# The memory's values first, the residual and the memory's parts kept in DRAM, and the first output units by heads

## The chip, the cores and the metric

The kernel runs on one core of a Trainium2 chip. The metric is the device time of one execution, in microseconds. Engines are named as the profile names them: PE (TensorE matmuls), PEld (its weight loads), DVE (VectorE), ACT (ScalarE), POOL (GpSimd), SP (SyncE, which issues the DMAs here). Each engine works through its own instructions in program order and waits on semaphores for the others.

## The reference

One layer over 256 tokens of width 1024: a mixer of four branches, a cross-attention into 256 memory tokens, and a mixture of 32 experts, each followed by a layer norm of alpha times the residual plus the branch.

```python
h = layer_norm(x, ln0)                       # "LN0"
z = h @ w_in + b_in                          # 36 column blocks of 256
h = layer_norm(alpha*h + mixer(z) @ w_out + b_out)
q = h @ ca_wq;  k = mem @ ca_wk;  v = mem @ ca_wv
o = softmax(q k^T / sqrt(256)) v             # 4 heads of 256
h = layer_norm(alpha*h + o @ ca_wo)
h = layer_norm(alpha*h + moe(h))             # top 4 of 32 experts
```

The values v depend only on the memory and on ca_wv, on nothing that the layer computes before.

## The kernel before

**Units.** All dense products before the experts are a queue of units (class `Unit`, L142). A unit is one weight block of 1024 x 256: `load` (L147) issues its 1 MiB on SP into one of three raw buffers; `split` (L153) makes the high part by an ACT cast (L162) and the low part as raw minus high, the first 640 columns of 2048 on POOL (L164) and the other 1408 on DVE (L166), into one of three ring slots W0 to W2. The run is 48 matmuls in two halves: high by high (L135), high by low (L137), low by high (L139), each over 8 k-blocks.

**Order.** `step` (L197) drives the queue: before unit i it issues the load of unit i+4 and the split of unit i+3 at the latest, and between the halves `advance` lets every chain (a generator with the elementwise work of a branch) go one yield further. What stands in an engine's row is fixed when the program is built; a load on SP that waits for its buffer holds all DMAs behind it.

**Stages.** The front: x is loaded, LN0 runs on DVE and ACT, 16 transposes (L235) bring it to columns, parts hT_hi and hT_lo are made, and the first in-unit starts. The mixer: 36 in-units and 8 branch units beside the chains of the branches. The middle: `chain_mem` (L851) loads memT, x again and three broadcast rows (ln0_g, ln0_b, b_out), splits memT into memT_hl (slot X), and rebuilds the residual h: subtract and scale on DVE (L861), times ln0_g (L862) and plus ln0_b (L864) on POOL, times alpha plus b_out on DVE (L868). Then the units k0, out0 to out3, k1 to k3, q0 to q3, v0 to v3 (L902), o0 to o3 (L922). `chain_att` (L1186) does one head: scores (L1192), max (L1195), exponentials (L1197), normalization (L1199), then, once that head's values are there, the transposes of the probabilities (L1206) and the product with the values vm (L1214), whose parts go to oT_hl (slot A).

**Experts.** Their weights, 128 tiles of 2 MiB (L1051) and 128 of 1 MiB (L1060), come over the same SP queue into rings of big slots (E, X, W1, W2, W0, A) and small slots (f, k, m, raw0, raw1, v, n, b), each as soon as its slot is free. `load_experts(2)` after the first attention steps issues one big tile into E and one small one into f; `load_experts(3)` four steps later goes on with X.

```python
    step(4)
    load_experts(2)
    step(4)
    load_experts(3)
```

Of the kernel before, what the change touches and what calls it, by code (L numbers as in the profile page):

```python
# [7 lines left out]
F32 = mybir.dt.float32  # L8
F32R = mybir.dt.float32r
# [11 lines left out]
NT = 2  # L21
# [30 lines left out]
def hybrid_layer_kernel(ctx: ExitStack, tc: tile.TileContext, t, dbg=None):  # L52
# [19 lines left out]
    def slot(where, shape, name, dt=F32):  # L72
        return slots[where].tile(shape, dt, tag=where, name=name)
# [6 lines left out]
    def by_k(pair):  # L80
        return tuple(a.rearrange("p (k t) -> p k t", k=KD) for a in pair)
# [9 lines left out]
    xs = ctx.enter_context(ExitStack())  # L91
    xp = xs.enter_context(tc.tile_pool(name="xp", bufs=1, side="right"))

    xt = [xp.tile([P, D], F32, tag="xt", bufs=2, name=f"xt{i}") for i in range(NT)]
    for i in range(NT):
        S.dma_start(xt[i], xrow[:, i, :])
    cols = cp.tile([P, NCOL], F32, name="cols")
# [44 lines left out]
    class Unit:  # L142
# [151 lines left out]
    prime(1, 0)  # L294
    S.dma_start(cols, t["cols"])
    prime(2, 0)
# [9 lines left out]
    norm(xt[1], *mr0[1])  # L306
    prime(2, 1)
    to_cm(xt[0], 0, hTf, "ln0g", "ln0b")
    to_cm(xt[1], 1, hTf, "ln0g", "ln0b", lambda: pz.tile([P, 4, P], F32, tag="z", name="ps_tr"))
# [5 lines left out]
    A.activation(warm, eps, AF.Sigmoid)  # L315
    xs.close()
# [485 lines left out]

    NMIX = len(queue)

    def until(n):
        step(n - st_["done"])
# [4 lines left out]
    chains.append(chain_b0())  # L811
    until(4)
    pms[:] = [(pmm, "mm")]
    conv[0] = chain_conv()
    chains.append(conv[0])
    until(7)
    chains.append(chain_c())
    until(16)
    chains.append(chain_d())
    until(18)  # L820
    sil_ready.append(1)
    merged = slot("m", [P, KD, T], "merged")
    until(20)
    xc_.close()
# [16 lines left out]
    def bcast(name):  # L841
        o = p3.tile([P, D], F32, tag="bcast", name="bc_" + name, bufs=4)
        S.dma_start(o, t[name].rearrange("(o d) -> o d", o=1).to_broadcast([P, D]))
        return o

    mf = slot("f", [P, KD, T], "memT_f")
    mx = mTh, mTl = by_k(hi_lo("X", "memT_hl"))
    h = slot("h", [P, NT, D], "h")
    st1 = [p3.tile([P, 4, 6], F32, tag="st", bufs=4, name=f"st1{n}") for n in range(NT)]

    def chain_mem():  # L851
        S.dma_start(mf, t["memT"])
        S.dma_start(h, xrow)
        g0, b0, bo = bcast("ln0_g"), bcast("ln0_b"), bcast("b_out")
        for q in range(4):
            yield
            yield
            sl = slice(2 * q, 2 * q + 2)
            split(mf[:, sl, :], mTh[:, sl, :], mTl[:, sl, :])
            if q < 2:  # L860
                V.tensor_scalar(h[:, q, :], h[:, q, :], *mr0[q], ALU.subtract, ALU.mult)  # L861
                G.tensor_tensor(h[:, q, :], h[:, q, :], g0, ALU.mult)  # L862
            else:
                G.tensor_tensor(h[:, q - 2, :], h[:, q - 2, :], b0, ALU.add)  # L864
        yield
        for n in range(NT):
            yield
            V.scalar_tensor_tensor(h[:, n, :], h[:, n, :], ALPHA, bo, ALU.mult, ALU.add)  # L868

# [31 lines left out]

    def unit_v(q):  # L902
        def run(w):
            ps = psum()
            tm(ps, 0, w, mx, KD)
            yield
            tm(ps, 1, w, mx, KD)
            V.tensor_copy(vm[:, :, q * 256:(q + 1) * 256], ps)
            v_done.append(q)
        queue.append(Unit(t["ca_wv"][q], KD, 256, run))  # L910

    def half(ps, n, w, ks, first, last):
# [9 lines left out]
    def unit_o(q):  # L922
        def run(w):
            ps = [psum()[:, 0, :] for _ in range(NT)]
            if q == 0:

                half(ps[0], 0, w, range(6), True, False)
                yield
                half(ps[1], 1, w, range(6), True, False)
                for n in range(NT):  # L930
                    half(ps[n], n, w, range(6, 8), False, True)
                    eva_o(q, n, ps[n])
            elif q == 1:
                for n in range(NT):
                    half(ps[n], n, w, range(8), True, True)
                    eva_o(q, n, ps[n])
                    if n == 0:
                        yield
            elif q == 2:
# [242 lines left out]
    qT = slot("m", [P, KD, T], "qT")  # L1182
    v_done = []
    oT = []

    def chain_att(hd):  # L1186
# [12 lines left out]
        V.tensor_tensor(pr, pr, sm[:, :, None].to_broadcast([P, NT, T]), ALU.mult)  # L1199
        while hd not in v_done:  # L1200
            yield
        pt = p3.tile([P, 2, T], F32, tag="pt", name="pt", bufs=2)
# [14 lines left out]

    step(4)
    load_experts(2)
# [543 lines left out]
```

## Time and profile before

| | |
|---|---|
| median of 3 runs | 1427.59 us (1427.23 to 1428.79) |
| profiled execution | 1427.23 us, of which the span of the trace 1425.5 us |
| PE busy | 1263.8 us (89%) |
| DVE, ACT, POOL busy | 531.7, 314.2, 232.7 us |
| mean DMA rate over the span | 338 GB/s, 482.04 MB in all |
| first in-unit's first matmul | 14.02 us |
| attention's V units | 419.69 to 450.60 us |
| first expert tile into a unit's ring slot (W1) issued | 466.90 us |

The span is cut into stages by what they wait for: up to about 465 us PE is nearly always busy and DMA is not, from there to the end DMA is full and PE is not. Groups of rows below are cited by number; a "window" is a stretch of the span with each engine's busy time in it, PEclk is the granted TensorE clock (1.00 is 2.4 GHz, 0.50 is 1.2 GHz).

### The profile page before, as it was taken

Reading aid. Unit: us, or ns where it says so; the run is one execution under the profiler, and the core shown is the slowest. Engines: PE = TensorE matmul, PEld = TensorE weight load, DVE = VectorE, ACT = ScalarE, POOL = GpSimd, SP = SyncE. Lnnn points to the kernel's source line nnn. Section 1 sums busy time; section 2 is a strip of 40 time slices with the busy share of each in tenths; the row PEclk is TensorE's granted clock in tenths of the full one; section 3 lists DMA queues with packets and bytes.
Section 4 is the critical chain, followed back from the end, with each engine's and each line's share of the span. In section 5 each row is a group of like instructions: output and inputs, shape, how many; then the busy total and the mean of one; then the engine's idle time right before and its main releaser. Section 6 shows DMA issues by size and latency. Waiting matters only on the chain. (4 is left out here: it accounts for less than half of the span.)

```text
span 1425.5 us, 18505 instructions
## 1 busy us (share of the span) xinstructions
PE 1263.8 (89%) x7677; PEld 739.9 (52%) x7677; DVE 531.7 (37%) x830; ACT 314.2 (22%) x433; POOL 232.7 (16%) x143
## 2 busy tenths in 40 slices
PE   6999999989999999877999799799899978976764
PEld 6989898978999743311443343344244322322111
DVE  5587779978944522111031121121113111211113
ACT  4475574453643300000000000000000000000001
POOL 6233144559653200000000000000000000000000
PEclk9999999998999999988999999999899998999987
DMA  6353334556575999999999999999999999999994
GB/s 235 119 178 119 119 119 163 187 227 203 182 271 211 385 429 405 424 423 425 427 425 425 424 423 427 425 426 424 425 427 425 425 424 425 426 425 426 424 420 204
DMA packets 51979, 482.04 MB, mean 338 GB/s; under 512 B 7840, under 2 KB 8240, under 8 KB 10704
## 3 DMA queue, kind: packets, MB, share of 16 engines
q1 hardware_dynamic: 51888, 480.79, 82.6%
q8 instruction: 62, 1.02, 0.3%
q14 instruction: 29, 0.24, 0.0%
HBM read 479.72 MB, written 1.05 MB: 337 GB/s over the span
## 5 line engine op out<-in xcount | busy, mean ns | idle before, releaser
L1471 PE MATMUL ps_h<-w,xg 128*32 128x512 f32 (+2 forms) x2048 | 418.3, 638 | 64.2 <-DMA w<-in_moe_w 59.5
L1471 PEld LDWEIGHTS ps_h<-w,xg 128*32 128x32 f32 (+2 forms) x2048 | 133.6, 134 | 325.0 <-issue 219.0
L1534 PE MATMUL ps_y<-w,at 128*32 128x512 f32 (+2 forms) x1024 | 214.2, 631 | 38.0 <-DMA w<-in_moe_w 37.4
L1480 DVE TENSOR_SCALAR act<-ps_h 128x512 f32<-128x512 f32 (+1 forms) x36 | 24.7, 687 | 497.9 <-PE ps_h L1471 497.8
L164 POOL TENSOR_TENSOR w_hl<-w_f,w_hl 128x640 fp32r<-128x640 f32 (+1 forms) x64 | 162.3, 2540 | 226.0 <-ACT w_hl L162 213.1
L1676 POOL TENSOR_TENSOR r<-r,gb 128x512 f32<-128x512 f32 x2 | 3.0, 1492 | 926.5 <-ACT r L1675 926.5
L1534 PEld LDWEIGHTS ps_y<-w,at 128*32 128x32 f32 (+2 forms) x1024 | 62.8, 133 | 166.9 <-issue 83.7
L166 DVE TENSOR_TENSOR w_hl<-w_f,w_hl 128x1408 fp32r<-128x1408 f32 x63 | 117.4, 1866 | 69.1 <-ACT w_hl L162 66.1
L162 ACT CAST w_hl<-w_f 128x2048 fp32r<-128x2048 f32 x63 | 120.0, 1906 | 103.9 <-DMA w_f<-in_w_in 36.0
L1518 ACT COPY ta<-ps_sc 128x256 f32<-128x256 f32 (+1 forms) x32 | 11.8, 369 | 472.8 <-PE ps_sc L1516 472.8
L379 DVE SCALAR_TENSOR_TENSOR convacc<-u,cols,convacc 128x256 f32<-128x256 f32 x120 | 90.2, 752 | 2.5
L135 PE MATMUL ps_mm<-hT_hi,w_hl 128*128 128x256 f32 x512 | 74.7, 289 | 5.5 <-ACT hT_hi L311 2.3
L1555 PE MATMUL acc<-y,ta 32*128 32x512 f32 (+2 forms) x256 | 73.6, 641 | 5.0 <-DVE y L1544 4.0
L139 PE MATMUL ps_mm<-hT_hi,w_hl 128*128 128x256 f32 x512 | 73.7, 287 | 2.5 <-POOL w_hl L164 1.8
L137 PE MATMUL ps_mm<-hT_lo,w_hl 128*128 128x256 f32 x512 | 74.0, 288 | 0.0
L135 PEld LDWEIGHTS ps_mm<-hT_hi,w_hl 128*128 128x128 f32 x512 | 66.9, 193 | 8.5 <-issue 3.1
L139 PEld LDWEIGHTS ps_mm<-hT_hi,w_hl 128*128 128x128 f32 x512 | 67.6, 196 | 3.2 <-POOL w_hl L164 2.2
L137 PEld LDWEIGHTS ps_mm<-hT_lo,w_hl 128*128 128x128 f32 x512 | 67.6, 196 | 0.6 <-DVE hT_lo L314 0.6
L1342 PEld LDWEIGHTS ps_g<-sg,h 128*128 128x128 f32 x416 | 50.5, 198 | 12.2 <-issue 8.3
L1342 PE MATMUL ps_g<-sg,h 128*128 128x128 f32 x416 | 53.0, 286 | 0.3
L1481 ACT ACTIVATE sg<-act 128x512 f32<-128x512 f32 (+1 forms) x36 | 22.7, 631 | 135.3 <-DVE act L1480 134.1
L1555 PEld LDWEIGHTS acc<-y,ta 32*128 32x128 f32 (+2 forms) x256 | 26.0, 194 | 30.8 <-issue 19.1
(397 smaller groups left out, 1242.8 us busy)
## 6 DMA issues: line engine op xcount, KB each, us to landing
w<-in_moe_w SPq DMA_DIRECT2D x128, 2048.0 KB, 29.4
w<-in_moe_w SPq DMA_DIRECT2D x128, 1024.0 KB, 29.5
w_f<-in_w_in SPq DMA_DIRECT2D x36, 1024.0 KB, 4.9
w_f<-in_w_branch SPq DMA_DIRECT2D x8, 1024.0 KB, 4.9
w_f<-in_ca_wk SPq DMA_DIRECT2D x4, 1024.0 KB, 4.9
w_f<-in_w_out SPq DMA_DIRECT2D x4, 1024.0 KB, 5.0
w_f<-in_ca_wq SPq DMA_DIRECT2D x4, 1024.0 KB, 5.0
w_f<-in_ca_wv SPq DMA_DIRECT2D x4, 1024.0 KB, 4.9
```

Source lines behind the costliest of these rows:

```text
L135: PE.matmul(out, wh(i), xh(i), start=first and i == ks[0], stop=False)
L137: PE.matmul(out, wh(i), xl(i), start=False, stop=False)
L139: PE.matmul(out, wl(i), xh(i), start=False, stop=last and i == ks[-1])
L162: A.copy(hi, self.raw)
L164: G.tensor_tensor(lo[:, :n], self.raw[:, :n], hi.bitcast(F32)[:, :n], ALU.subtract)
L166: V.tensor_tensor(lo[:, n:], self.raw[:, n:], hi.bitcast(F32)[:, n:], ALU.subtract)
L379: V.scalar_tensor_tensor(ca[:, c, :], u[:, c, j:j + T], col("caw", 4 * j + c), ca[:, c, :], ALU.mult, ALU.add)
L1342: PE.matmul(pss[k // 4][:, k % 4 * w:(k % 4 + 1) * w], h[:, n, feature_tile(0, k)], sg[:, n, :w], start=n == 0 and k % 4 == 0, stop=n == N ...
L1471: PE.matmul(up_out(cap, hp_, m, i), x[:, k, :], w[:, c:c + 512], start=False, stop=k == KD - 1, skip_group_check=True)
L1480: V.tensor_scalar(g, hg, LIMIT, None, ALU.min)
L1534: PE.matmul(o, at[:, k, :], w[:, q * 512:(q + 1) * 512], start=k < (2 if cap == 32 else 1), stop=k >= KD - (2 if cap == 32 else 1), skip_g ...
L1555: PE.matmul(acc[n][q], a, b, start=False, stop=last, skip_group_check=True)
```

## The change

Line numbers of the new kernel are given as L.. "after". The memory's transpose is loaded first of all, in two halves, then wv0, x, the column constants, wv1, wv2, the three broadcast rows; memT is split at once, its parts are stored to DRAM (s_mem, 2 MiB, L329 after). The queue begins with the four V units; they run as steps 1 to 4 between the parts of LN0: V0, V1, the transposes, V2, V3, then in0. Each V unit's result is copied by ACT and stored to s_v (L305 after). The residual is finished here (POOL times ln0_g L344, plus ln0_b L352; DVE L353) and stored to s_h (L354 after). `chain_mem` is gone; the middle loads h, memT_hl and, later, vm from DRAM (4 MiB where it was 3.5 MiB). The attention has no V units between q3 and o0. The big ring begins X, A, W1, W2, W0, E, and oT_hl lies in E; `load_experts(2)` stands four steps earlier. Unit o0 does o0 and o1 together, by heads: k-blocks 0 to 3, then 4 and 5, then 6 and 7 of both.

```diff
+    s_mem = dp.tile([P, 2, KD * T], F32, name="s_mem")
+    s_v = dp.tile([P, NT, D], F32, name="s_v")
+    s_h = dp.tile([P, NT, D], F32, name="s_h")
+    mf = xp.tile([P, KD, T], F32, name="memT_f")
+    for i in range(2):
+        S.dma_start(mf[:, 4 * i:4 * i + 4, :], t["memT"][:, 4 * i:4 * i + 4, :])
...
+    def unit_v(q):
+        def run(w):
+            ps = psum()
+            tm(ps, 0, w, mx, KD)
+            yield
+            tm(ps, 1, w, mx, KD)
+            vs = xp.tile([P, 2, T], F32, tag="vs", name="vs", bufs=2)
+            A.copy(vs, ps)
+            S.dma_start(s_v[:, :, q * 256:(q + 1) * 256], vs)
+        queue.append(Unit(t["ca_wv"][q], KD, 256, run))
...
+    for q in range(4):
+        unit_v(q)
     for q in range(2):
         unit_in(q, eva_v(q))
...
+    for q in range(4):
+        sl = slice(2 * q, 2 * q + 2)
+        split(mf[:, sl, :], mTh[:, sl, :], mTl[:, sl, :])
+    prime(3, 1)
+    S.dma_start(s_mem, mhl.bitcast(F32))
+    step(1)
...
+    step(1)
     to_cm(xt[0], 0, hTf, "ln0g", "ln0b")
...
+    for n in range(NT):
+        G.tensor_tensor(xt[n], xt[n], row0[0], ALU.mult)
+    step(1)
...
+    for n in range(NT):
+        G.tensor_tensor(xt[n], xt[n], row0[1], ALU.add)
+        V.scalar_tensor_tensor(xt[n], xt[n], ALPHA, row0[2], ALU.mult, ALU.add)
+        S.dma_start(s_h[:, n, :], xt[n])
+    step(1)
...
+    S.dma_start(h, s_h)
+    S.dma_start(mhl.bitcast(F32), s_mem)
...
-    def chain_mem():
...
+    S.dma_start(vm, s_v)
...
-    big = ["E", "X", "W1", "W2", "W0", "A"]
+    big = ["X", "A", "W1", "W2", "W0", "E"]
...
-        while hd not in v_done:
-            yield
+        yield
...
+                part(range(4), parts[:1])
                 yield
...
+                part(range(4), parts[1:])
+                advance()
+                part(range(4, 6), parts[:2])
+                advance()
+                part(range(4, 6), parts[2:])
+                part(range(6, 8), parts)
...
-    step(4)
     load_experts(2)
     step(4)
     load_experts(3)
```

Three places show how this orders the instructions. First SP at the start of the program, before, down to the first small constants (wlr):

```order
L96 DMA xt_78<-in_x 128x1024
L96 DMA xt_79<-in_x 128x1024
L151 DMA w_f<-in_w_in 128x2048
L295 DMA cols<-in_cols 128x292
L151 DMA w_f<-in_w_in 128x2048 x3
L351 DMA wlr<-in_w_lr 128x128
```

And SP of the changed kernel, from the store of the memory's parts on (memT, x, the columns, wv0 to wv2 and the rows stand ahead of it):

```order
L329 DMA s_mem<-memT_hl 128x4096
L157 DMA w_f<-in_ca_wv 128x2048
L305 DMA s_v<-vs 256x1x256
L157 DMA w_f<-in_w_in 128x2048
L305 DMA s_v<-vs 256x1x256
L157 DMA w_f<-in_w_in 128x2048
L305 DMA s_v<-vs 256x1x256
L354 DMA s_h<-xt_86 128x1024
L354 DMA s_h<-xt_87 128x1024
L157 DMA w_f<-in_w_in 128x2048
L305 DMA s_v<-vs 256x1x256
L157 DMA w_f<-in_w_in 128x2048
```

The load of the third in-unit's weights (the third `in_w_in`) now stands behind both stores of the residual. Second, POOL at the start, before: one split, then the constants.

```order
L164 TENSOR_TENSOR w_hl<-w_f,w_hl 128x2048
L321 MEMSET ones 128x128
L323 MEMSET nones 128x128
L325 AFFINE_SELECT ntri<-nones 128x128
L328 CAST identb<-ident 128x128
```

And POOL of the changed kernel at the same place:

```order
L169 TENSOR_TENSOR w_hl<-w_f,w_hl 128x640 x4
L344 TENSOR_TENSOR xt_86<-xt_86,bc_ln_g 128x1024
L344 TENSOR_TENSOR xt_87<-xt_87,bc_ln_g 128x1024
L169 TENSOR_TENSOR w_hl<-w_f,w_hl 128x640
L352 TENSOR_TENSOR xt_86<-xt_86,bc_ln_b 128x1024
L352 TENSOR_TENSOR xt_87<-xt_87,bc_ln_b 128x1024
L169 TENSOR_TENSOR w_hl<-w_f,w_hl 128x640
L361 MEMSET ones 128x128
```

The four V units' splits and the residual's four operations stand ahead of the constants, between them the splits of in0 and in1. Third, SP in the attention, before:

```order
L151 DMA w_f<-in_ca_wq 128x2048 x4
L151 DMA w_f<-in_ca_wv 128x2048 x3
L1051 DMA w_4277<-in_moe_w 128x4096
L1060 DMA w_4279<-in_moe_w 128x2048
L151 DMA w_f<-in_ca_wv 128x2048
L151 DMA w_f<-in_ca_wo 128x2048 x3
L1051 DMA w_4561<-in_moe_w 128x4096
L151 DMA w_f<-in_ca_wo 128x2048
```

And in the changed kernel:

```order
L157 DMA w_f<-in_ca_wq 128x2048 x3
L1068 DMA w_4257<-in_moe_w 128x4096
L1077 DMA w_4259<-in_moe_w 128x2048
L157 DMA w_f<-in_ca_wq 128x2048
L157 DMA w_f<-in_ca_wo 128x2048 x3
L1068 DMA w_4553<-in_moe_w 128x4096
L157 DMA w_f<-in_ca_wo 128x2048
```

The first two expert tiles (3 MiB) stood ahead of the last V unit's weights; now they stand ahead of the last q unit's.

## Rows read from the trace of the kernel before

**Rows 1.** Busy time by window: `us, PE (x) PEld DVE ACT POOL, PEclk, DMA share, GB/s`
```profile
445.00:450.00 5.00, 5.00 (x38) 4.79 (x37) 2.26 (x2) 0.59 (x1) 2.97 (x1) 1.00 0.01 3
...
600.00:1400.00 800.00, 692.26 (x3446) 261.07 (x3446) 136.47 (x269) 50.70 (x95) 0.00 (x0) 0.95 1.01 425
```

**Rows 2.** Timeline of SP's issues, attention: start, us, engine, line, op, tile, [idle <-releaser]
```profile
392.70 3.24 SPq L151 DMA_DIRECT2D w_f<-in_ca_wq  x2
...
451.23 0.37 SPq L151 DMA_DIRECT2D w_f<-in_ca_wo  x1
...
466.90 0.43 SPq L1051 DMA_DIRECT2D w<-in_moe_w  x1
```

**Rows 3.** Timeline of the first 30 us, columns as in rows 2
```profile
8.35 3.33 PE L235 MATMUL ps_tr<-ident,xt 128*128 128x128 f32 x16 [8.35 <-DVE l0rs L124]
...
9.04 1.04 ACT L158 CAST w_hl<-w_f 128x1024 fp32r<-128x1024 f32 x1 [1.38 <-DMA w_f<-in_w_in]
...
14.02 0.74 PE L135 MATMUL ps_mm<-hT_hi,w_hl 128*128 128x256 f32 x4 [2.35 <-ACT hT_hi L311]
...
14.63 0.20 POOL L321 MEMSET ones<- 128x128 f32 x1
...
15.58 1.22 PE L135 MATMUL ps_mm<-hT_hi,w_hl 128*128 128x256 f32 x4 [0.82 <-DVE hT_hi L311]
...
22.71 3.11 POOL L164 TENSOR_TENSOR w_hl<-w_f,w_hl 128x640 fp32r<-128x640 f32 x2
...
23.95 1.12 PE L135 MATMUL ps_mm<-hT_hi,w_hl 128*128 128x256 f32 x8
```

**Rows 4.** A window in the first unit, columns as in rows 1
```profile
18.00:19.00 1.00, 1.00 (x5) 0.97 (x5) 1.00 (x1) 1.00 (x1) 1.00 (x2) 0.50 0.93 374
```

**Rows 5.** The four V units' matmuls in their window, columns as in rows 1
```profile
419.69:450.60 30.91, 24.83 (x192) 23.42 (x192) 0.00 (x0) 0.00 (x0) 1.00 0.51 197
```

**Rows 6.** Timeline, POOL's part of a split, without DVE beside it and with
```profile
37.70 1.57 POOL L164 TENSOR_TENSOR w_hl<-w_f,w_hl 128x640 fp32r<-128x640 f32 x1 [1.87 <-ACT w_hl L162]
...
306.70 2.99 POOL L164 TENSOR_TENSOR w_hl<-w_f,w_hl 128x640 fp32r<-128x640 f32 x1 [2.18 <-ACT w_hl L162]
```

**Rows 7.** Operations on tile h, middle stage: duration ns min/median/max, starts
```profile
L862 POOL TENSOR_TENSOR h<-h,bc_ln_g x2: 2403/3042/3680, 302.1 to 314.6; 128x1024 f32<-128x1024 f32 x2
...
L864 POOL TENSOR_TENSOR h<-h,bc_ln_b x2: 2814/2834/2853, 320.7 to 326.4; 128x1024 f32<-128x1024 f32 x2
```

**Rows 8.** PE's waits, 300 to 345: waited for, us in total, times, longest
```profile
PE ps_mm L135 <- ACT merged_hl L128: 2.8, 2, 1.6
...
PE ps_mm L137 <- DVE yl L129: 2.7, 1, 2.7
```

**Rows 9.** Windows of the middle stage, columns as in rows 1
```profile
320.00:324.00 4.00, 3.81 (x19) 3.52 (x18) 4.00 (x2) 0.00 (x0) 4.00 (x3) 0.50 0.52 168
...
344.00:348.00 4.00, 4.00 (x20) 4.00 (x20) 2.18 (x3) 1.86 (x2) 3.71 (x13) 0.50 0.98 258
```

**Rows 10.** Timeline of the attention, ACT, DVE, POOL and PE, columns as in rows 2
```profile
397.57 1.90 ACT L162 CAST w_hl<-w_f 128x2048 fp32r<-128x2048 f32 x1 [6.68 <-DMA w_f<-in_ca_wq]
...
400.61 1.90 ACT L162 CAST w_hl<-w_f 128x2048 fp32r<-128x2048 f32 x1 [0.64 <-DMA w_f<-in_ca_wq]
...
403.77 1.12 PE L139 MATMUL ps_mm<-h1T_hl,w_hl 128*128 128x256 f32 x8
...
404.73 1.12 PE L135 MATMUL ps_mm<-h1T_hl,w_hl 128*128 128x256 f32 x8
...
406.06 0.69 DVE L1199 TENSOR_TENSOR pr<-pr,sm 128x512 f32<-128x512 f32 x1
...
460.86 1.90 ACT L162 CAST w_hl<-w_f 128x2048 fp32r<-128x2048 f32 x1 [5.14 <-DMA w_f<-in_ca_wo]
...
464.28 1.12 PE L135 MATMUL ps_mm<-w_hl,oT_hl 128*128 128x256 f32 x8
```

More of the change, by code (lines that the diff above doesn't have):

```diff
@@ L91, in hybrid_layer_kernel @@
     xs = ctx.enter_context(ExitStack())
[L92 removed]
+    xp = xs.enter_context(tc.tile_pool(name="xp", bufs=1, side="right", reuse_waits="tile"))
+    dp = ctx.enter_context(tc.tile_pool(name="scratch", bufs=1, space=bass.MemoryType.DRAM))
+    s_mem = dp.tile([P, 2, KD * T], F32, name="s_mem")
[4 more added lines that the diff above has]
+        S.dma_start(mf[:, 4 * i:4 * i + 4, :], t["memT"][:, 4 * i:4 * i + 4, :])
     xt = [xp.tile([P, D], F32, tag="xt", bufs=2, name=f"xt{i}") for i in range(NT)]
[L95 to L96 removed]
     cols = cp.tile([P, NCOL], F32, name="cols")
@@ L294, in hybrid_layer_kernel @@
     prime(1, 0)
+    for i in range(NT):
+        S.dma_start(xt[i], xrow[:, i, :])
     S.dma_start(cols, t["cols"])
-    prime(2, 0)
+    prime(3, 0)
+    row0 = [xp.tile([P, D], F32, name="bc_" + n) for n in ("ln0_g", "ln0_b", "b_out")]
+    for o, n in zip(row0, ("ln0_g", "ln0_b", "b_out")):
+        S.dma_start(o, t[n].rearrange("(o d) -> o d", o=1).to_broadcast([P, D]))
     warm = xp.tile([P, 1], F32, name="warm")
     A.activation(warm, eps, AF.Sqrt)
+    for q in range(4):
[4 more added lines that the diff above has]
+    step(1)
     mr0 = []
@@ L801, in hybrid_layer_kernel @@
                 unit_wb(n, hf, i == 0)
-    NMIX = len(queue)
+    NMIX, NV = len(queue), st_["done"]
     def until(n):
@@ L811, in hybrid_layer_kernel @@
     chains.append(chain_b0())
-    until(4)
+    until(NV + 4)
     pms[:] = [(pmm, "mm")]
@@ L815, in hybrid_layer_kernel @@
     chains.append(conv[0])
-    until(7)
+    until(NV + 7)
     chains.append(chain_c())
-    until(16)
+    until(NV + 16)
     chains.append(chain_d())
-    until(18)
+    until(NV + 18)
     sil_ready.append(1)
     merged = slot("m", [P, KD, T], "merged")
-    until(20)
+    until(NV + 20)
     xc_.close()
@@ L841, in bcast @@
     def bcast(name):
-        o = p3.tile([P, D], F32, tag="bcast", name="bc_" + name, bufs=4)
+        o = p3.tile([P, D], F32, tag="bcast", name="bc_" + name, bufs=2)
         S.dma_start(o, t[name].rearrange("(o d) -> o d", o=1).to_broadcast([P, D]))
         return o
-    mf = slot("f", [P, KD, T], "memT_f")
-    mx = mTh, mTl = by_k(hi_lo("X", "memT_hl"))
+    mhl = slot("X", [P, 2, KD * T], "memT_hl", F32R)
+    mx = by_k((mhl[:, 0, :], mhl[:, 1, :]))
     h = slot("h", [P, NT, D], "h")
+    S.dma_start(h, s_h)
+    S.dma_start(mhl.bitcast(F32), s_mem)
     st1 = [p3.tile([P, 4, 6], F32, tag="st", bufs=4, name=f"st1{n}") for n in range(NT)]
-    def chain_mem():
[L852 to L855, printed above, removed]
-            yield
[L857 to L868, printed above, removed]
     def unit_k(q):
@@ L923, in run, with part @@
         def run(w):
-            ps = [psum()[:, 0, :] for _ in range(NT)]
+            ps = [psum()[:, 0, :] for _ in range(NT)] if q % 2 == 0 else None
             if q == 0:
-                half(ps[0], 0, w, range(6), True, False)
-                yield
[L929 to L938, printed above, removed]
+                w2 = (w, queue[st_["done"] + 1].w)
+                pss = (ps, [psum()[:, 0, :] for _ in range(NT)])
+                parts = [(i, n) for i in range(2) for n in range(NT)]
+                def part(ks, which):
+                    for i, n in which:
+                        half(pss[i][n], n, w2[i], ks, ks[0] == 0, ks[-1] == KD - 1)
+                        if ks[-1] == KD - 1:
+                            eva_o(i, n, pss[i][n])
+                part(range(4), parts[:1])
+                yield
+                part(range(4), parts[1:])
[4 more added lines that the diff above has]
+                part(range(6, 8), parts)
             elif q == 2:
@@ L1182, in hybrid_layer_kernel @@
     qT = slot("m", [P, KD, T], "qT")
-    v_done = []
     oT = []
```

23 lines of the change are left out of this document (5 added, 18 removed).

## The prediction

> **What bounds the kernel now.** I read the table of slices first, then windows, then the timelines of the three stretches that the change touches. From 600 to 1400 DMA is full at 425 GB/s while PE works 692 of 800 us [rows 1]: this part ends a fixed number of bytes after it begins. Just ahead of it, in 445 to 450, PE works all of 5 us and DMA moves 3 GB/s [rows 1]: there PE's chain decides. The two meet where the first expert tile into slot W1 is issued, at 466.90 [rows 2]; from then on tiles follow without a gap. So the time moves with this issue: what the change takes from or adds to PE's chain before 466.90 counts in full, and what it saves in the transfers before it counts nothing. I therefore add up three shifts of that issue: front, middle, attention. Sums are made on the profiled execution (1427.23, span 1425.5, so 1.73 outside the trace); the median of the runs is 0.36 above it.
>
> **The front: V units ahead of the in-units.** Before, the first weights land at 9.04, but the first in-unit waits for LN0 and its parts until 14.02; the second starts at 23.95 [rows 3]. A unit is six groups of eight matmuls, each starting 0.96 us after the last (403.77 and 404.73 [rows 10]), 5.76 us. The first took 9.93: 0.82 is one wait [rows 3], the rest, 3.35, is the clock, granted at 0.50 in a window of it [rows 4]. I take 3.4 as the price of one cold spell.
>
> Now V0 needs only memT (1 MiB, as x was) and wv0, which lands at the place of the first weights: start 9.04 + 1.04 (the cast) = 10.1. It is the first unit of a cold engine: with 9.93 it ends at 20.0. Then V1, V2 and V3 (3 x 5.76), the transposes (3.33 [rows 3], between V1 and V2) and in0 (5.76): the second in-unit starts at 46.4 instead of 23.95, +22.4. The V units' 23.0 us (4 x 5.76; their busy time with modelled ends is 24.83 [rows 5]) are paid here; the start is 3.9 earlier, but the transposes' 3.3, which lay in the first wait, now lie between the units.
>
> Then POOL, in its new order. V1 ends at 25.8, the transposes at 29.1; only then may ln0_g be multiplied into x: 2 x 3.04, to 35.2; in0's low part 3.0, to 38.2; ln0_b twice, 2.83 each, to 43.9 [rows 6, 7]. DVE's last step of the residual takes some 1.6 (the other operations of such size are 0.8 to 2.8), to 45.5, and only then can SP issue the second store, and behind it the load of the third in-unit. 1 MiB lands 4.9 us after its issue on an idle queue (392.70 to 397.57 [rows 2, 10]), and the second store's half MiB and part of the first lie ahead, about 2.5: 52.9. Cast 1.9, to 54.8. The third in-unit should begin at 52.2: 2.6 late. Its low part on POOL stands also behind the constants (8.1 us, 14.63 to 22.71 [rows 3]), and comes 3.0 after the cast, at 57.8 to 58.0, where the third pass wants it 1.92 after the unit's start, 56.7: 1.2 more. That is 3.8, and a pause of this size lets the clock fall about every second time: +1.7. The front's value is 22.4 + 3.8 + 1.7 = **+28**; bounds +21.6 (nothing late, V0 without the 0.8 that its like waited) and +31 (the multiplications at 3.68, the full cold spell).
>
> On the POOL prices: a split part takes 1.57 alone and 2.99 beside DVE's part [rows 6]. The Trainium skill (SBUF — State Buffer, "SBUF: two separate sides") says that DVE and GpSimd share one port pair under an exclusive lock, so that the loser waits for the whole instruction. The trace agrees (2.99 is about its 1.57 and a DVE part of 1.63 one after the other), and by that rule each of the residual's four operations would add its own length to DVE's parts too; the front would come out 2 to 3 us above my value, which lies in its bounds.
>
> The stores themselves (2 MiB, 1 MiB, 1 MiB) lie beside PE's work, and the added bytes cost nothing where DMA has room.
>
> **The middle: `chain_mem` goes.** POOL loses 2 x 3.04 + 2 x 2.83 = 11.7 us [rows 7], DVE and ACT the splits. PE waited here 2.7 for yl and 2.8 for merged_hl [rows 8], each with a half-clock spell behind it (0.50 in 320 to 324 and 344 to 348 [rows 9]). The yl wait stands beside chain_mem's POOL operation, so it and its cold spell go: -6.1. The second pair isn't chain_mem's: merged_hl waits for POOL's merging, and 1 MiB (vm) now stands ahead of the router's rows: I let it stay. Value **-6**, bounds -2.7 (the yl wait alone) and -12.3 (both waits and both spells).
>
> **The attention: V units out, two expert tiles earlier.** 23.0 us of matmuls leave. But they covered two waits. First, head 0's probabilities: they are ready at 406.06 + 0.69 = 406.75, while PE is through with q1 at 404.73 [rows 10]. Before, V units and q2, q3 lay between; now PE's next instruction after q1 is their transpose, 2.0 late even if nothing else moves. Second, what delays them. DVE's low part of q3 and ACT's cast of q3 stand ahead of head 0's max and exponentials. Before, q3's weights landed at 400.61 [rows 10]. Now X and f (3 MiB) stand between q2's load and q3's on SP, and k3, which frees X, is done before q2's load. From q2's landing at 397.57, 4 MiB (4.19 MB) at 425 GB/s take 9.9: q3 lands at 407.4, 6.8 later, and the probabilities come at 413.6. That a load behind a tile comes late is in the trace: wo3, issued at 451.23 behind one tile of 2 MiB, is cast at 460.86, 9.6 later [rows 2, 10]. PE stands still from 404.7 to 413.6, 8.9, and the clock falls, 3.4.
>
> Last, the tail. Before, o3's cast at 460.86 started 6.0 ahead of the W1 issue, which came 2.6 after o1's last group (464.28 starts o2 [rows 10]). Now o0 and o1 end together, o3's split may begin only when o0's ring slot is free, 1.4 (12 matmuls of 0.12) before that: issue 4.6 after o1, so 2.0 later.
>
> Sum -23.0 + 8.9 + 3.4 + 2.0 = **-8.7**, bounds -21.0 (only the 2.0 of the softmax) and -5.3 (a second cold spell, since every head's softmax now has one half unit of 2.9 us to hide in).
>
> **Sum.** +28 - 6 - 8.7 = +13.3: the profiled execution would take 1440.5, runs' median **1441**.
>
> **A rule of the skill against the estimate of the loads.** The trace's rate is 425 GB/s [rows 1]. The Trainium skill (DMA: Bandwidth & Descriptors, "Specifications") gives a limit of about 358 GB/s of memory bandwidth for one core; here the measurement decides. By the page's figure q3 would land 1.8 us later (11.7 for the 4.19 MB), and the sum would be near 1443.
>
> **Rivals.**
> A, the queue doesn't bite. If small loads overtake tiles (the 16 DMA engines work on several transfers at once), or X is free only after q3's load is out, q3 lands in time, and in front the third in-unit's load is not held either. Front +22.4, middle -6.1, attention -21.0: -4.7, 1422.9. It decides from the point where q3's weights land within 5 us of their issue and PE goes from the second in-unit to the third without a gap. For it: DMA moves 3 GB/s in places, so room is there. Against: wo3's 9.6.
> B, only the attention's wait is covered and the front's stall is there: +28 - 6 - 21 = +1, 1428.9. For it: the 8.9 rest on an order of ACT and DVE that one late landing decides. Against: the row of wo3 again.
> C, every pause is followed by a cold clock and POOL runs at its contended prices: +31 - 2.7 - 5.3 = +23, 1450.6. For it: both cold spells of the middle followed pauses of under 3 us.
>
> **How the numbers follow.** My forecast has 0.52, with a range of its own from 1432 to 1449; A has 0.22, B 0.13, C 0.13. What a measurement of this kernel can tell from no change is 0.2%, 2.9 us: faster is below 1424.7, slower above 1430.5. Of A some 0.16 lies below (0.06 within), of B 0.02 below and 0.07 within; the forecast's own lower end adds 0.01 to each. Faster 0.19, same 0.14, slower 0.67. The range, 1422 to 1452, leaves out about the lower third of A and the top of C.
>
> **What would show it.** The second in-unit's first matmul at 46 to 47; a wait of PE at the third in-unit on its cast, near 52 to 55; no wait for yl in the middle; q3's cast 7 us or more after the issue; PE idle ahead of head 0's transposes, released by the probabilities; the W1 issue at 477 to 482. I am wrong if in1 starts before 43 or after 52, if the transposes wait less than 4 us, or if the time after the W1 issue, now 958.6, changes by more than 2 us.

## The result, and the profile after

The changed kernel takes 1445.9 us in the median of its runs (1443.6 to 1449.9), the kernel before 1427.4 in those of the same series: a ratio of 1.0129, 95% interval 1.0114 to 1.0144, so slower by 18.5 us. The profiled execution took 1449.85 (span 1448.2), the slowest of the four; its W1 issue comes 23.2 later than before, its span is 22.7 longer. What follows the issue is unchanged: 1448.2 - 490.05 = 958.2, before 958.6.

Where the time went is read by following the same matmuls through both traces: the lag of a group behind its twin. Rows of the kernel before, beside those of [rows 2, 10]: the two subtractions that make hT_lo, then three matmul groups (the low-rank product that follows the third in-unit, out0's second half, one of q0); columns are start, us, engine, line, operation, [idle before <- releaser]:

```profile
15.45 2.52 DVE L314 TENSOR_TENSOR hT_lo<-hT_f,hT_hi 128x1024 fp32r<-128x1024 f32 x2
...
35.47 1.09 PE L135 MATMUL ps_lr<-hT_hi,wlr_hi 128*16 128x256 f32 x8
...
347.64 1.79 PE L135 MATMUL ps_mm<-w_hl,merged_hl 128*128 128x256 f32 x8
...
392.73 1.22 PE L139 MATMUL ps_mm<-h1T_hl,w_hl 128*128 128x256 f32 x8 [0.55 <-POOL w_hl L164]
```

The twins of the three groups in the changed kernel, then those of 404.73 and 464.28 and, last, of the W1 issue:

```profile
68.25 1.09 PE L141 MATMUL ps_lr<-hT_hi,wlr_hi 128*16 128x256 f32 x8
...
368.87 1.12 PE L141 MATMUL ps_mm<-w_hl,merged_hl 128*128 128x256 f32 x8
...
424.63 1.22 PE L145 MATMUL ps_mm<-h1T_hl,w_hl 128*128 128x256 f32 x8 [2.03 <-POOL w_hl L169]
...
446.58 2.06 PE L141 MATMUL ps_mm<-h1T_hl,w_hl 128*128 128x256 f32 x8
...
485.29 1.12 PE L141 MATMUL ps_mm<-w_hl,oT_hl 128*128 128x256 f32 x8
...
490.05 5.26 SPq L1068 DMA_DIRECT2D w<-in_moe_w  x2
```

| stage | lag at its end | the stage's own part | forecast |
|---|---|---|---|
| front (68.25 against 35.47) | +32.8 | +32.8 | +28 |
| mixer and middle up to out0 (368.87, 347.64) | +21.2 | -11.6 | |
| the rest of the middle (424.63, 392.73) | +31.9 | +10.7 | middle in all: -6 (measured -0.9) |
| q0 to the transposes of head 0 (446.58, 404.73) | +41.9 | +10.0 | |
| to o2 (485.29, 464.28) | +21.0 | -20.8 | |
| to the W1 issue (490.05, 466.90) | +23.2 | +2.1 | attention in all: -8.7 (measured -8.7) |

**The front of the changed kernel**, first the starts of V0 and of wv3's way, then in0, the second in-unit, PE's waits for hT_lo (us in all, times, longest) and the third in-unit's cast:

```profile
10.05 2.07 PE L141 MATMUL ps_mm<-w_hl,memT_hl 128*128 128x256 f32 x8 [10.05 <-ACT w_hl L164]
...
13.07 0.33 SPq L157 DMA_DIRECT2D w_f<-in_ca_wv  x1
...
29.10 1.91 ACT L167 CAST w_hl<-w_f 128x2048 fp32r<-128x2048 f32 x1 [5.03 <-DMA w_f<-in_ca_wv]
...
32.59 1.36 DVE L245 TENSOR_SCALAR hT_f<-ps_tr,cols 128x128 f32<-128x128 f32 x4
...
39.07 0.74 PE L141 MATMUL ps_mm<-hT_hi,w_hl 128*128 128x256 f32 x4
...
41.64 6.10 POOL L352 TENSOR_TENSOR xt<-xt,bc_ln_b 128x1024 f32<-128x1024 f32 x2
...
42.14 6.68 DVE L350 TENSOR_TENSOR hT_lo<-hT_f,hT_hi 128x1024 fp32r<-128x1024 f32 x2
...
55.87 1.12 PE L141 MATMUL ps_mm<-hT_hi,w_hl 128*128 128x256 f32 x8
...
PE ps_mm L143 <- DVE hT_lo L350: 4.6, 2, 2.6
...
59.28 1.91 ACT L167 CAST w_hl<-w_f 128x2048 fp32r<-128x2048 f32 x1 [17.94 <-DMA w_f<-in_w_in]
```

V0 starts at 10.05, as worked out. But in0, begun at 39.07, ends only at 55.87: 16.8 us for a unit of 5.76. Of the 11.0 too much, 2.5 are a wait for hT_hi and 4.6 the two for hT_lo; most of the rest is the half clock behind them (granted 0.68 in the mean of 40 to 56, below). wv3's load is issued at 13.07 and cast 16 us later. Its cast on ACT and its low part on DVE stand ahead of the copies of LN0's columns (hT_f, 32.59), though the transposes had been done since 27.4, and so the parts of hT are made late: two subtractions take 6.68 us (42.14), since POOL's additions (41.64) run beside them; before, the two took 2.52 (15.45). The third in-unit's weights are cast at 59.28, and by then in0's delay has covered most of that: PE waits 0.6 there, for POOL's part.

PE's clock in in0, and in the 10 us after the attention's wait (columns as in rows 1):

```profile
40.00:56.00 16.00, 9.09 (x46) 8.59 (x47) 14.17 (x7) 1.34 (x2) 15.66 (x16) 0.68 0.24 77
...
446.00:456.00 10.00, 10.00 (x54) 9.58 (x54) 4.58 (x4) 1.89 (x3) 1.56 (x1) 0.76 0.57 202
```

**The middle.** PE's waits from 300 to 400 (waited for: us in all, times, longest):

```profile
PE ps_mm L143 <- POOL w_hl L169: 4.3, 2, 2.5
...
PE ps_mm L141 <- ACT w_hl L167: 1.4, 1, 1.4
...
PE ps_mm L143 <- DVE yl L135: 0.3, 1, 0.3
```

The waits for yl and merged_hl [rows 8] are nearly gone (0.3, in a second profile of this kernel too). But in no_resid, wv3_first, x_after_q3 and vm_late below, whose mixer is the changed kernel's, the wait for yl is 1.7 to 1.8, without any `chain_mem`; so a part of what is won here comes and goes. The place of these waits is taken by waits for POOL's and ACT's parts of out1 and out2. The rows behind them, the issue of out2's and out3's loads, out1's low part on POOL, PE's wait for it, and out2's cast:

```profile
367.49 8.16 SPq L157 DMA_DIRECT2D w_f<-in_w_out  x2
...
373.74 1.53 POOL L169 TENSOR_TENSOR w_hl<-w_f,w_hl 128x640 fp32r<-128x640 f32 x1
...
375.33 1.83 PE L143 MATMUL ps_mm<-w_hl,merged_hl 128*128 128x256 f32 x8 [2.46 <-POOL w_hl L169]
...
381.37 1.90 ACT L167 CAST w_hl<-w_f 128x2048 fp32r<-128x2048 f32 x1 [12.53 <-DMA w_f<-in_w_out]
```

POOL goes from the merge straight into 8 us of constants, and out1's low part is ready at 375.3, 2.46 after PE asks for it. out2's cast comes at 381.37 for another reason: its load is issued at 367.49, behind vm, the router's rows and the experts' biases, and lands 13.8 us later (the loads use two raw buffers in turn, and the one that out1's low part frees is out3's, issued at 375.30). The 10.7 us of lag that come back by q0 stand mainly in these waits, on half clock in part (granted 0.50 in 377 to 379), and in the wait of 2.03 for q0's low part (424.63).

**The attention.** SP's issue of q3's load, q2's cast, q3's cast, and PE's wait for head 0's probabilities:

```profile
426.13 0.50 SPq L157 DMA_DIRECT2D w_f<-in_ca_wq  x1
...
429.57 1.91 ACT L167 CAST w_hl<-w_f 128x2048 fp32r<-128x2048 f32 x1 [8.25 <-DMA w_f<-in_ca_wq]
...
439.56 1.90 ACT L167 CAST w_hl<-w_f 128x2048 fp32r<-128x2048 f32 x1 [7.59 <-DMA w_f<-in_ca_wq]
...
445.84 1.08 PE L1221 MATMUL ps_pt<-ident,pr 128*128 128x128 f32 x4 [8.96 <-DVE pr L1215]
```

q3 is cast 10.0 us after q2 (forecast 9.9), and PE stands 8.96 us (forecast 8.9). By the figure of about 358 GB/s in the Trainium skill (DMA: Bandwidth & Descriptors, "Specifications") q3's cast would, as an estimate, have stood 11.7 after q2's; the measurement decides for the rate of the rows, 425.

### The profile page after: what moved, and what is told of

Same layout as the page of the kernel before. It is cut to its first block, busy times and chain, and to the rows that moved or that the text cites. A ratio compares the mean times of both kernels' runs of the same rounds, so it can differ in the third digit from the quotient of the medians.

```text
span 1448.2 us, 18537 instructions
## 1 busy us (share of the span) xinstructions
PE 1272.6 (88%) x7677; PEld 745.8 (52%) x7677; DVE 529.0 (37%) x825; ACT 316.6 (22%) x437; POOL 227.0 (16%) x143
## 5 line engine op out<-in xcount | busy, mean ns | idle before, releaser
L1548 PE MATMUL ps_y<-w,at 128*32 128x512 f32 (+2 forms) x1024 | 219.5, 649 | 38.8 <-DMA w<-in_moe_w 38.0
L169 POOL TENSOR_TENSOR w_hl<-w_f,w_hl 128x640 fp32r<-128x640 f32 x64 | 159.0, 2488 | 262.1 <-ACT w_hl L167 252.9
L1356 PEld LDWEIGHTS ps_g<-sg,h 128*128 128x128 f32 x416 | 54.3, 211 | 14.7 <-issue 10.5
L1356 PE MATMUL ps_g<-sg,h 128*128 128x128 f32 x416 | 56.8, 299 | 0.5 <-DVE act L1501 0.3
L1495 ACT ACTIVATE sg<-act 128x512 f32<-128x512 f32 (+1 forms) x36 | 22.7, 631 | 135.5 <-DVE act L1494 134.4
## 6 DMA issues: line engine op xcount, KB each, us to landing
w<-in_moe_w SPq DMA_DIRECT2D x128, 2048.0 KB, 29.4
```

The source lines that it names most:

```text
L1356: PE.matmul(pss[k // 4][:, k % 4 * w:(k % 4 + 1) * w], h[:, n, feature_tile(0, k)], sg[:, n, :w], start=n == 0 and k % 4 == 0, stop=n == N ...
L1548: PE.matmul(o, at[:, k, :], w[:, q * 512:(q + 1) * 512], start=k < (2 if cap == 32 else 1), stop=k >= KD - (2 if cap == 32 else 1), skip_g ...
```

## The experiments

All but one do the whole of the computation. Medians stand against the changed kernel's 1445.95 (eight runs in two series) and the kernel before (1428.0 to 1428.7 in their series).

**again**: the changed kernel, unchanged.

> The changed kernel once more, for a second profile, since its four runs lie between 1443.6 and 1449.9. The stages of the first profile, as the lag of the same matmul behind the kernel before: +32.7 at the fourth in-unit, +31.9 at the first q unit, +21.0 at the first matmul of o2, +23.2 at the W1 issue. If the difference between its runs is made by PE's clock in the pauses, a faster run shows the same waits with fewer or shorter half-clock stretches, 2 to 5 us less in one stage; if it is made by the DMA stream, the lag at the W1 issue is the same and the time after it differs from 958.

Measured 1445.9 (1443.1 to 1446.6), span 1444.6.

```profile
422.09 1.12 PE L145 MATMUL ps_mm<-h1T_hl,w_hl 128*128 128x256 f32 x8
...
486.50 11.87 SPq L1068 DMA_DIRECT2D w<-in_moe_w  x4
```

The lag is the same through the front and the mixer to within 0.5, and 3.5 less at the W1 issue (19.6). 2.5 of it is there at the group of q0 (422.09, a lag of 29.4), just before which the first profile has the wait of 2.03 for POOL's low part of q0 (424.63). Its longer pauses at out2 aren't in it: at q0's first group the two are 0.35 apart (420.53 and 420.18), since the second profile waits 4.9 for LN1's h where the first waits 2.0. The time after the issue is 958.1. So the two differ in pauses of the middle, not in the stream, and the first profile has the middle some 2.5 worse.

**no_resid**: the residual's arithmetic left out of the front (the residual is therefore not the reference's).

```diff
-    for n in range(NT):
-        G.tensor_tensor(xt[n], xt[n], row0[0], ALU.mult)
...
-        G.tensor_tensor(xt[n], xt[n], row0[1], ALU.add)
-        V.scalar_tensor_tensor(xt[n], xt[n], ALPHA, row0[2], ALU.mult, ALU.add)
```

> The changed kernel without the residual's arithmetic in the front (POOL's four operations and DVE's two; the stores stay, and the residual is wrong). Theory 1: the front's excess over the 22.4 of the units themselves comes from POOL's operations holding up DVE while it makes in0's parts hT_hi and hT_lo. Then in0 takes some 9 us instead of 16.8, the second in-unit starts near 47.5 to 49 instead of 55.9, and the time falls by 7 to 9 us against the changed kernel. Theory 2, the prediction's own: what costs is the third in-unit's load behind the two stores on SP and its low part behind the constants on POOL. Then the second in-unit still starts near 55.9, the third starts at once as it did, and the time hardly moves.

Measured 1440.7, 5.2 less (7 to 9 expected). DVE's two hT_lo and the second in-unit's start:

```profile
41.23 3.79 DVE L348 TENSOR_TENSOR hT_lo<-hT_f,hT_hi 128x1024 fp32r<-128x1024 f32 x2
...
51.28 1.12 PE L141 MATMUL ps_mm<-hT_hi,w_hl 128*128 128x256 f32 x8
```

The two subtractions take 3.79 instead of 6.68, and the second in-unit starts at 51.28 instead of 55.87. Theory 1 holds in kind, and for less than it said: the second in-unit's lag is 31.9, which is 9.5 over its units' 22.4, and 4.6 of these 9.5 come from the residual's arithmetic. The prediction's place, the third in-unit, lies behind this point and wasn't it. The time alone would not tell: without the arithmetic the stores, and behind them the third in-unit's load, go out early too (40.79).

**resid_late**: all work done, POOL's constants at the very start, the residual's second half after in0, its store issued by ACT.

```diff
-    step(1)
+    step(2)
+    for n in range(NT):
+        G.tensor_tensor(xt[n], xt[n], row0[1], ALU.add)
+        V.scalar_tensor_tensor(xt[n], xt[n], ALPHA, row0[2], ALU.mult, ALU.add)
+        A.dma_start(s_h[:, n, :], xt[n])
     xs.close()
```

> The changed kernel with POOL's constants at the very start of the program, and the residual's second half (plus ln0_b, alpha, b_out, store) after in0 instead of ahead of it; the store is issued by ACT. All work is done. Theory 1 (collision of POOL with DVE in the making of hT_lo): in0's waits for hT_lo, 4.6 us in all, shrink to under 1 and the second in-unit starts near 49 to 51 (the multiplications still lie beside DVE's work): 5 to 7 us less than the changed kernel. Theory 2 (SP's and POOL's order at the third in-unit): nothing is gained at the second in-unit, and at most 1 at the third. A third reading, that POOL's work only moves: it then holds the fourth in-unit's low part, and the lag at the sixth unit is again over 30.

Measured 1441.7, 4.2 less.

```profile
42.17 3.70 DVE L374 TENSOR_TENSOR hT_lo<-hT_f,hT_hi 128x1024 fp32r<-128x1024 f32 x2
...
52.58 1.12 PE L141 MATMUL ps_mm<-hT_hi,w_hl 128*128 128x256 f32 x8
```

hT_lo takes 3.70, PE's wait for it is 1.7 (4.6 before, under 1 expected), and the second in-unit starts at 52.58, 3.3 earlier (5 to 7 expected).

**wv3_first**: the rows' loads and the memory's store behind wv3's load and behind those of the first in-units.

```diff
     norm(xt[1], *mr0[1])
     step(1)
+    for o, n in zip(row0, ("ln0_g", "ln0_b", "b_out")):
+        S.dma_start(o, t[n].rearrange("(o d) -> o d", o=1).to_broadcast([P, D]))
...
     step(1)
+    S.dma_start(s_mem, mhl.bitcast(F32))
```

> The changed kernel with the three broadcast rows and the store of the memory's parts issued on SP behind the loads of wv3 and the first in-units instead of ahead of wv3 (3.5 MiB fewer ahead of it). Theory: in the front what is late is wv3 (issued 13.1, cast at 29.1), and since its cast and low part stand ahead of the copies of LN0's columns on ACT and DVE, hT_hi and hT_lo come late, and in0 takes 16 us. Then wv3 is cast by 21, the columns are copied at 27 to 31, in0 waits under 3 us, the second in-unit starts at 46 to 50 and the time falls by 5 to 8 against the changed kernel's 1446. Rival: the residual's operations on POOL hold up DVE in any case, so the columns' parts are still late, and under 3 us are gained. Second rival: without wv3 late, the in0 weights are late instead, and in0 waits for its own cast.

Measured 1444.2, 1.8 less (5 to 8 expected; 1438.7 to 1447.3, the profile is of the slowest run), which the spread of the changed kernel's own runs (1443.1 to 1449.9) doesn't tell from nothing. wv3's cast, the second in-unit, SP's load for the third one, and PE's wait:

```profile
23.94 1.89 ACT L167 CAST w_hl<-w_f 128x2048 fp32r<-128x2048 f32 x1
...
50.57 1.12 PE L141 MATMUL ps_mm<-hT_hi,w_hl 128*128 128x256 f32 x8
...
50.89 0.39 SPq L157 DMA_DIRECT2D w_f<-in_w_in  x1
...
PE ps_mm L141 <- ACT w_hl L167: 2.5, 1, 2.5
```

wv3 is cast at 23.94 instead of 29.10, and the second in-unit starts at 50.57, 5.3 earlier. Now the prediction's step shows: the third in-unit's load stands behind the residual's stores, is issued at 50.89, and PE waits 2.5 for its cast; the lag, 26.6 at the second unit, is 30.2 in the third. The two causes stood one behind the other, and the first hid the second.

**x_after_q3**: the first two expert tiles behind q3's weights.

```diff
-    load_experts(2)
-    step(4)
+    step(1)
+    load_experts(2)
+    step(3)
     load_experts(3)
```

> The changed kernel with the first two expert tiles (X and f, 3 MiB) issued after q3's weights instead of ahead of them. Theory: the 3 MiB hold q3's weights by 7 us, ACT's cast and DVE's low part of q3 stand ahead of head 0's softmax, and PE waits 8.96 for it and then runs on half clock. Then q3's cast comes 5 us after its issue, the wait for head 0's probabilities falls to about 2, no half clock follows, and the W1 issue moves 9 to 11 us earlier: 1435. Rival: what is in the way is only moved, and the 3 MiB now hold wo0's weights, for which o0 waits: then a wait for wo0's parts of 3 to 7 us stands at o0, and the time falls by 3 to 6 at most. Second rival: the chain of heads (2.7 us of softmax for one half unit) binds anyway: then the wait for head 0 stays at 5 or more.

Measured 1438.5, 7.4 less (9 to 11 expected). q0's first group, q3's cast, the transposes of head 0, the W1 issue:

```profile
423.44 1.12 PE L141 MATMUL ps_mm<-h1T_hl,w_hl 128*128 128x256 f32 x8
...
431.54 1.90 ACT L167 CAST w_hl<-w_f 128x2048 fp32r<-128x2048 f32 x1 [0.57 <-DMA w_f<-in_ca_wq]
...
437.83 0.63 PE L1221 MATMUL ps_pt<-ident,pr 128*128 128x128 f32 x4 [0.99 <-DVE pr L1215]
...
480.52 11.88 SPq L1068 DMA_DIRECT2D w<-in_moe_w  x4
```

The wait of 8.96 is now 0.99, q3 is cast 3.0 after q2, and wo0's lateness costs nothing: no wait stands at o0. Against the second profile the W1 issue is 6.0 earlier and the span 7.7 shorter. In the attention the gain is larger: from q0's first group to the W1 issue it takes 57.1, where the second profile takes 66.3 (from 420.18); q0 began 3.3 later here, behind a middle that waited for yl again.

**vm_late**: the reload of the values after k1 to k3.

```diff
-    S.dma_start(vm, s_v)
...
+    S.dma_start(vm, s_v)
     qT = slot("m", [P, KD, T], "qT")
```

> The changed kernel with the reload of the values (1 MiB) issued after the units k1 to k3 instead of ahead of the router's rows. Theory: of the 12.4 us that the middle wins up to the first out unit, some 8 to 10 are lost again at out1 and out2, part of it since vm delays the router's rows and out2's weights. Then out2's weights come 2 to 3 us earlier, the wait of 1.4 to 1.8 for them goes, and the lag at the first q unit falls by 2 to 4 (1442 to 1444). Rival: POOL's chain of constants after the merge, 8 us ahead of out1's low part, binds: then the wait of 2.5 for it stays and under 1 is gained.

Measured 1444.9, 1.0 less (2 to 4 expected), which the spread of the changed kernel's runs doesn't tell from nothing. POOL's wait in the middle, and the attention's:

```profile
PE ps_mm L143 <- POOL w_hl L169: 1.4, 1, 1.4
...
PE ps_pt L1221 <- DVE pr L1215: 10.6, 1, 10.6
```

out2's cast is no longer waited for, and out1's low part 1.4 instead of 2.5; but the 1 MiB now stands ahead of q3's weights, and the wait for head 0 grows from 8.8 to 10.6. q0 begins 1.8 earlier than in the second profile (418.34 and 420.18), and the transposes of head 0 at the same time (442.38 in both): what the middle wins is paid there.

**all_mended**: the four orders above together.

```diff
+    step(2)
...
+        A.dma_start(s_h[:, n, :], xt[n])
...
+    S.dma_start(vm, s_v)
     qT = slot("m", [P, KD, T], "qT")
...
+    step(1)
     load_experts(2)
-    step(4)
+    step(3)
```

> The changed kernel with all orders mended: POOL's constants first, wv3 ahead of the rows and the memory's store, the residual's second half after in0, vm reloaded late, X and f after q3's weights. If the gains add (front 8 to 10, middle 2, attention 7.5), 1426 to 1429: about as fast as before, and then moving the values bought nothing by itself: the V units cost 23 in the front, and save 20 to 21 in the attention. Rival: the front's second half stays, since in0 is still late by its columns: 1430 to 1436. Second rival: below 1424, where the middle's gain comes through in full.

Measured 1433.7 (1430.7 to 1435.2; 1426 to 1429 expected, 1430 to 1436 by the first rival), a ratio to before of 1.0035 (1.0022 to 1.0047): 12.2 less than the changed kernel, where the four alone sum to 14.4, and still slower than before.

```profile
PE ps_pt L1220 <- DVE pr L1214: 3.1, 1, 3.1
...
39.45 1.11 PE L141 MATMUL ps_mm<-hT_hi,w_hl 128*128 128x256 f32 x8
...
48.85 1.12 PE L141 MATMUL ps_mm<-hT_hi,w_hl 128*128 128x256 f32 x8
```

V3 ends where it did (in0 starts at 39.45), in0 takes 9.4 with 3.1 of waits for hT_lo, which DVE makes beside two of POOL's splits (2.58 and 2.56 us, 1.30 each before). The second in-unit starts 24.9 later than before: with the orders mended the front pays the V units' 23 and a little more. 2.3 go on top at the low-rank product, in a wait for wlr's high part, which ACT makes behind the residual's store. In the attention a wait of 3.1 for head 0 is left.

**resid_only**: the kernel before, with the residual moved (computed after in0, stored to DRAM, reloaded in the middle) and, to make room for it on POOL, POOL's constants to the start of the program; memory and V units stay.

```diff
+        A.dma_start(s_h[:, n, :], xt[n])
...
-        S.dma_start(h, xrow)
-        g0, b0, bo = bcast("ln0_g"), bcast("ln0_b"), bcast("b_out")
+        S.dma_start(h, s_h)
```

> The kernel before, with only the residual taken out of the middle: POOL's constants at the very start, the residual computed after in0 and stored to DRAM by ACT, h reloaded from there; memT and its parts, and the V units, where they were. Theory: the middle's wait for yl and the half clock behind it came from chain_mem's residual on POOL and DVE; without it the middle wins 4 to 8 by out0, of which POOL's constants give half back, and the front pays 0 to 2: 1421 to 1426 against 1428. Rival: what is won in the middle is given back wholly at out1 and out2 (as in the changed kernel): 1427 to 1429. Second rival: the residual after in0 delays the fourth in-unit's low part: slower, 1430 or more.

Measured 1424.0, a ratio of 0.9966 (0.9955 to 0.9977): faster. out0's second half is 9.5 us earlier than before, and the waits for yl and merged_hl are 0.5 and 0.2; ACT, standing at the store, made wlr's parts late (3.4 of wait), and 3.9 of the 9.5 go again by the W1 issue (461.34). The gain stands in the middle, where the residual was; what the constants' move does by itself no run shows.

**resid_m**: the same, the residual's last step written to the free slot m, and stored by SP after the fourth in-unit.

```diff
+    hm = slot("m", [P, NT, D], "h_pre")
...
-        A.dma_start(s_h[:, n, :], xt[n])
...
     until(4)
+    S.dma_start(s_h, hm)
```

> The kernel before with the residual in the front, as in the run that had only that, but its last step written to the free slot m and stored by SP after the fourth in-unit, so that ACT waits for nothing. Theory: the 3.4 us wait for wlr's parts and what follows it (a lag of 2.7 at the low-rank product, 5 in the mixer) came from ACT standing at the store; without it the front is level with the kernel before, and the W1 issue comes 8 to 10 us earlier: 1418 to 1421. Rival: the lag in the mixer is of another cause (POOL's or DVE's row), and the time stays at 1423 to 1425.

Measured 1420.5, a ratio of 0.9942 (0.9926 to 0.9957): the fastest here. Waits in the front and the middle, and the W1 issue:

```profile
PE ps_lr L141 <- DVE wlr_lo L131: 3.0, 1, 3.0
...
PE ps_mm L139 <- POOL w_hl L166: 2.3, 1, 2.3
...
PE ps_mm L139 <- DVE yl L131: 0.6, 1, 0.6
...
459.99 13.79 SPq L1052 DMA_DIRECT2D w<-in_moe_w  x4
```

Its time is as expected, its reason only in part: the wait in the front is still there, 3.0, now for the part that DVE makes behind the residual's last step, and the W1 issue is 6.9 earlier than before (8 to 10 expected), only 1.4 earlier than in resid_only. The other 1.9 of the 3.2 between these two profiles lie behind the issue.

**const_late**: the same, and the second half of POOL's constants behind out1's and out2's low parts.

```diff
+        for j in range(3):
+            S.dma_start(b1f[32 * j:32 * j + 32, :], t["moe_b1"])
+        yield
+        yield
...
+        V.tensor_copy(rsum, ps)
+        yield
         G.iota(tie[:, :NE], pattern=[[-1, NE]], base=NE - 1, channel_multiplier=0, allow_small_or_imprecise_dtypes=True)
...
-        for j in range(3):
-            S.dma_start(b1f[32 * j:32 * j + 32, :], t["moe_b1"])
-        yield
-        yield
```

> The same, and the second half of POOL's constants (the tie and caps rows, some 3.5 us) moved behind out1's and out2's low parts. Theory: what the middle wins is partly given back at out1, because POOL's chain from the merge over the constants to out1's low part ends last there (2.3 to 2.5 of wait and a half-clock stretch after it). Then the wait goes, the lag at the q units improves by 3 to 4 against the same kernel without it: 1415 to 1418. Rival: out2's weights, which wait on SP for the buffer that out1's split frees and land behind the router's rows, set the pace: then a wait for them takes its place, and at most 1 us is gained.

Measured 1426.6, 6.1 slower than without it (3 to 4 faster expected). POOL's waits in the middle, and the first of the moved constants:

```profile
PE ps_mm L139 <- POOL w_hl L166: 5.5, 2, 3.7
...
349.45 3.73 POOL L1132 TENSOR_SCALAR_AFFINE_SELECT tie<-tie 32x1 f32<-32x1 f32 x2
```

out1's wait is gone, as the theory said, but the constants now run beside DVE (two of them 3.73 us; they took 0.42) and hold out3's low part, 3.7; the other 1.8 is out2's low part behind its late weights, the rival's wait. The work was moved to a worse place.

**o_by_heads**: the kernel before, with o0 and o1 by heads.

```diff
-                half(ps[0], 0, w, range(6), True, False)
+                part(range(4), parts[:1])
...
+                part(range(4), parts[1:])
+                advance()
+                part(range(4, 6), parts[:2])
+                advance()
+                part(range(4, 6), parts[2:])
+                part(range(6, 8), parts)
```

> The kernel before, with only the units o0 and o1 by heads. Theory: with the V units still there PE waits nowhere at o0, so the form wins nothing, and o3's split may begin only when o0's ring slot is free, near the end of both: the W1 issue comes some 4.6 after o1's last matmul instead of 2.6: 2 us slower, 1430 to 1431 against 1428.5. Rival: o3's weights land so late (behind a tile) that the split is not later than before: no difference (within 1 us). Second rival: o0's start is earlier by what its first parts don't need, and the time is 1 to 2 us shorter.

Measured 1427.7 against 1428.0, a ratio of 0.9992 (0.9982 to 1.0002): no difference.

```profile
471.16 11.88 SPq L1057 DMA_DIRECT2D w<-in_moe_w  x4
```

The W1 issue is 4.3 later than before, and the time isn't. 2.1 of the 4.3 are there when o0 begins (453.08, before 450.96), ahead of anything that the edit touches; the other 2.1 are the tail's 2.0 of the forecast. What follows the issue is 2.4 shorter in this profile, and the run stood above its median. So this issue marks the end only to within 3 us (what follows it is 955.9 to 959.7 in the profiles here), and in the time the tail's 2.0 isn't shown.

## Why the prediction was right, and where its sizes were off

- **The number and the signs.** The direction and the range came true, but not by a good sum: in the profile the issue moved by 23.2 where the sum has 13.3, with front and middle both outside their bounds, to the same side. That the median, 4.9 above the forecast, still lies in the range, and in the forecast's own of 1432 to 1449, is owed to their width. Of the signs, the second in-unit's start failed (55.87; 46 to 47 was named, and beyond 52 the prediction calls itself wrong), and so did the third in-unit's wait on its cast (0.6, on POOL's part) and the W1 issue (490.05; 477 to 482). The wait for yl, q3's cast (13.4 after its issue), the wait for head 0 and the time after the issue came as named.
- **What bounds.** Right: the time after the W1 issue stayed at 958.
- **The front** (+28, bounds +21.6 to +31; measured +32.8, above them). V0's start and duration and the end of V3 came as worked out (39.1; the terms gave 40.6, with transposes that ran faster). The step that failed is "in0 (5.76)": it took 16.8. I had every part of LN0 ready by then, since its inputs were long there, and hadn't followed which instruction stands ahead of hT's copies on ACT and DVE: wv3's split, whose weights come 16 us after their issue. That is the same trap that I had seen for q3. It is one of two causes: with wv3 early the second in-unit starts 5.3 earlier, without the residual's arithmetic 4.6, with both mended (all_mended) 7.0. The stall that I put at the third in-unit (3.8, and 1.7 as half a cold spell, for which the prediction shows no row) measured 0.6, being covered by in0's; it appeared (2.5) when wv3's lateness was taken away. The rule of the Trainium skill (SBUF — State Buffer, "SBUF: two separate sides"), by which DVE and GpSimd share a port pair that one of them holds for a whole instruction, agrees with the rows where the two engines met: 6.68 for two subtractions beside POOL's additions, 3.79 without them. I had named it, for 2 to 3 us, without seeing that it would fall on the making of in0's parts.
- **The middle** (-6; measured -0.9 in the first profile, some 2.5 better in the second). The gain up to out0 was 11.6, about twice the term, both waits and both cold spells; and 10.7 of it was given back from out1 to q0, for which the prediction has no term: it prices nothing on POOL behind the merge, and nothing for vm's MiB ahead of out2's weights. In resid_only 3.9 of 9.5 were given back by the W1 issue, in resid_m 3.1 of 10.0; there the middle loads 2 MiB, not 4, and the V units don't shift the loads.
- **The attention** (-8.7; measured -8.7, and -9.8 in the second profile): the 8.9 of wait (8.96) and its cause, shown by x_after_q3, were right. The tail's 2.0 is in the W1 issue (2.1, and 2.1 in o_by_heads) but, by o_by_heads, not shown in the time.
- **The rivals.** A and B, in which the queue doesn't bite, fell: q3's load behind 3 MiB came when 425 GB/s says. C was the nearest in the front (+31) and in the middle (-2.7; measured -0.9 and, in the second profile, -3.4), there by other waits than it names, and not in the attention; the median lies about halfway between its 1450.6 and the forecast's 1441. (B's sum of +1 gives 1428.6, not 1428.9.)
- **The value of the move itself.** No run moves the V units alone. The nearest pair is all_mended and resid_only, 1433.7 against 1424.0, which both store the residual from ACT (resid_m, which doesn't, has 1420.5); beside the V units' and the memory's place they differ in the expert tiles' order and in the form of o0 and o1. The rows agree with a loss: the 23 us of matmuls are paid in full in the front (24.9 in all_mended), where only 4 us of PE's wait were free, and their leaving the attention gains less, at best 19.7 (x_after_q3: 57.1 from q0's first group to the W1 issue, 76.8 before).

What stays open: how much of the middle's give-back in the changed kernel is vm's MiB and how much POOL's chain (vm_late and const_late each moved a wait instead of removing it), and why the wait for yl is 0.3 in both profiles of the changed kernel and 1.7 to 1.8 in four of the kernels made from it.

## What to carry to other kernels

Matmuls that are moved cost nothing only where PE idles at the new place, here for 4 us of 23. When a load is put behind others, ask not who uses its data but what stands behind its first consumer (the cast and the split) in the rows of ACT and DVE: here LN0's columns and head 0's softmax. A large change should be taken apart before it is judged: of this one the residual, moved to the front with POOL's constants out of its way, makes the kernel 0.6% faster.

## What the runs showed that I had not expected

Two DVE subtractions of 128x1024 took 2.5 us in the kernel before, 3.79 where one of POOL's splits of weights stood beside the first of them, and 6.68 beside POOL's additions; and a pair of POOL's 32x1 selects, 0.42 us in the kernel before, took 3.73 beside DVE's part of a split and its work on the experts' biases.
